# The second expert stage of a two-layer transformer kernel: float32 weights unsplit, two 64-column groups, 18 landing buffers

## The chip, the core and the metric

The kernel runs on one core of one Trainium2 chip. The metric is the device time of one execution in microseconds (us); lower is better. The core has a matrix engine (TensorE, PE in the profile, its weight loads as PEld), a vector engine (DVE), a scalar engine (ACT), GpSimd (POOL) and a queue engine (SP) that issues most DMAs. All of them run at once and wait for each other by semaphores.

## The reference

Two blocks run one after the other. The first has two layers (`DEPTH = 2`), each a mixer and then a mixture of 16 experts in which every expert picks its own tokens. In the second layer only the 512 latent tokens go through the experts, so each of the 16 experts takes 64 tokens of width 1024:

```python
def expert_choice_ffn(h, w_router, w_g, w_u, w_d):
    B, n, D = h.shape
    cap = CAPACITY_FACTOR * n // N_EXPERTS          # 2 * 512 / 16 = 64
    ...
    gate, idx = lax.top_k(aff, cap)
    xs = h[bi, idx]
    a = jnp.einsum('becd,edf->becf', xs, w_g)       # 1024 x 1024 weights per expert
    u = jnp.einsum('becd,edf->becf', xs, w_u)
    y = jnp.einsum('becf,efd->becd', jax.nn.silu(a) * u, w_d)
    return jnp.zeros_like(h).at[bi, idx].add(y * gate[..., None].astype(y.dtype))
```

Three weight matrices per expert make 48 matrices of 4 MB, 201.3 MB in float32, which are each read once.

## The kernel before

`experts(l, ...)` (L1080) is the expert stage of both layers. In layer 1 (the second) it works thus. The mixer before it has written the normed tokens to DRAM as `h2d` (`ffn_input`, L926: transposes `hpt` L992, ACT copies L998, POOL adds L999, four stores L1000), and `top_k` has made the `route` table on DVE. Then, for each expert:

- `gather` (L1128): an indirect DMA on POOL fetches 128 rows of `h2d` into `xs`. 64 of them are the expert's own tokens, the other 64 rows of the array are not used in this layer.
- `turned` (L1114): 8 PE transposes of 128x128 into PSUM, then an ACT copy to the high part and a DVE subtraction to the low part (both float32r, a rounded 32-bit format that PE multiplies in one pass).
- `product` (L1097): a 1024x1024 matrix comes in four loads of 1 MB (`eraw`, L1102, issued on SP, two rows of 4 KB per partition, 8 buffers in pool `er`). Each load is split by ACT (`eh`, L1105) and DVE (`el`, L1106), and then

```python
                    for i in range(2):
                        k = c * 2 + i
                        for f in range(2):
                            fs = slice(f * 512, f * 512 + 512)
                            self.mm3(ps[:, fs], xh[:, k, :], xl[:, k, :], h[:, i, fs], lo[:, i, fs], k == 0, k == 7)
```

  where `mm3` (L80 to L84) is three matmuls: high by high, high by low, low by high. That is 48 matmuls of 128x512 for each matrix. A load's buffer is free again when DVE has made `el`.
- The order of the products is up(e), gate(e+1), down(e), up(e+1). Between them lie SiLU on ACT (L1221), the product with `pup` on DVE (L1233) and another `turned` for the hidden values (`ath`, `atl`).
- `finish` (L1184) scales the output rows on ACT and DVE (`yp..`, L1142, L1143). After every fourth expert a generator `scatter` (L1150) is put in the background: 8 pieces of 128 output columns, each with 4 matmuls against one-hot matrices (L1165) and one DVE update of the residual `xL` (L1167). One piece runs after each step of later products. After the last piece the second block begins with its own weight loads (`raw`, L92) and products (`d`).

The Tile framework allocates buffers and orders each engine's instructions; every engine runs its own list strictly in order. SP's list holds all weight loads one behind the other, so a load that waits for a buffer holds back all that follow.

Of other code the prediction uses only `first_ada` (L462), whose loops issue 64 matmuls in plain float32 at L478, each of 2 stationary columns and 256 moving columns.

Of the kernel before, what the change touches and what calls it, by code (L numbers as in the profile page):

```python
# [9 lines left out]
F32 = mybir.dt.float32  # L10
# [60 lines left out]
class Kernel:  # L71
# [854 lines left out]
    def ffn_input(self, l, lat, T, x, h2d, row0):  # L926


        nc = self.nc
        i = 0 if lat else 1  # L930
        nt = T // 128
        A, B = self.mcol(l, i, 4), self.mcol(l, i, 3)
        u = self.op.tile([128, 8, T], F32, name="u", tag="o")
        w3 = self.tp.tile([128, 3, 8, NE], F32, name="wr", tag="hn", bufs=4)
        wr, wb = w3[:, 0], w3[:, 1:]
        nc.scalar.dma_start(wr, self.A["w_router"][l].rearrange("(k p) e -> p k e", p=128))
        nc.vector.tensor_mul(wb[:, 0], wr, B[:, :, None].to_broadcast([128, 8, NE]))
        nc.vector.tensor_reduce(wb[:, 1, 0], wb[:, 0].rearrange("p k e -> p e k"), axis=AX, op=ALU.add)
        row = [self.tp.tile([128, 512], F32, name="brow", tag="hn", bufs=4) for _ in range(2)]
        for hf in range(2):  # L940
            pb = self.pt.tile([128, 512], F32, name="bps", tag="t")
            for j in range(4):
                dg = self.sp.tile([128, 128], F32, name="diag", tag="diag", bufs=2)
                nc.vector.tensor_scalar(dg, self.ident, B[:, hf * 4 + j:hf * 4 + j + 1], None, ALU.mult)
                nc.tensor.matmul(pb[:, j * 128:j * 128 + 128], self.ones, dg, start=True, stop=True)
            nc.scalar.activation(row[hf], pb, AF.Copy)
        pb = self.pt.tile([128, 512], F32, name="bps", tag="t")
        nc.tensor.matmul(pb[:, :NE], self.ones, wb[:, 1, 0], start=True, stop=True)
        nc.vector.tensor_copy(wb[:, 1, 1], pb[:, :NE])
        acc = self.tp.tile([128, 512], F32, name="acc", tag="oj", bufs=1)[:, :T]  # L950
        lg = self.po.tile([128, 512], F32, name="o", tag="o")[:, :nt * NE].rearrange("p (t e) -> p t e", e=NE)

        def put(j):
            sq = acc if j == 0 else self.tp.tile([128, 512], F32, name="sq", tag="tmp", bufs=5)[:, :T]
            nc.scalar.activation(sq, x[:, j, :], AF.Square)
            if j:
                nc.vector.tensor_add(acc, acc, sq)
            nc.scalar.activation(u[:, j, :], x[:, j, :], AF.Copy, scale=A[:, j:j + 1])
            for t in range(nt):
                nc.tensor.matmul(lg[:, t], u[:, j, t * 128:t * 128 + 128], wr[:, j, :], start=j == 0 and t == 0,  # L960
                                 stop=j == 7 and t == nt - 1, skip_group_check=True)

        def finish():
            if lat:
                ps = self.ps.tile([128, 1024], F32, name="S", tag="S")
            else:
                ps = self.ps.tile([128, 512], F32, name="S", tag="Sc", bufs=2)
            for t in range(nt):
                nc.tensor.matmul(ps[:, t:t + 1], acc[:, t * 128:t * 128 + 128], self.ones[:, 0:1], start=True, stop=True)
            r = self.sp.tile([128, 4], F32, name="nrc", tag="nrc", bufs=2)  # L970
            self.rstd(r[:, :nt], ps[:, :nt], D)
            halves = self.cp.tile([128, nt // 2, 2, NE], F32, name="aff", tag=f"aff{i}")
            aff = halves.rearrange("p t h e -> p (t h) e")
            for t in range(nt):
                nc.vector.scalar_tensor_tensor(halves[:, t % (nt // 2), t // (nt // 2)], lg[:, t], r[:, t:t + 1], wb[:, 1, 1], ALU.mult, ALU.add)
            mx = self.sp.tile([128, 2, nt], F32, name="mx", tag="mx", bufs=1)
            nc.vector.tensor_reduce(mx[:, 0], aff, axis=AX, op=ALU.max)
            nc.vector.tensor_sub(aff, aff, mx[:, 0, :, None].to_broadcast([128, nt, NE]))
            nc.scalar.activation(aff, aff, AF.Exp)
            nc.vector.tensor_reduce(mx[:, 1], aff, axis=AX, op=ALU.add)  # L980
            nc.vector.reciprocal(mx[:, 1], mx[:, 1])
            nc.vector.tensor_mul(aff, aff, mx[:, 1, :, None].to_broadcast([128, nt, NE]))
            self.aff[i] = halves
            if i == 1 or l == 1:
                for _ in self.top_k(lat):
                    pass
            for t in range(nt):
                tok = self.tp.tile([128, 1024], F32, name="tok", tag="big", bufs=2)
                for hf in range(2):
                    ps = self.pt.tile([128, 512], F32, name="hpt", tag="t")  # L990
                    for j in range(4):
                        nc.tensor.transpose(ps[:, j * 128:j * 128 + 128], u[:, hf * 4 + j, t * 128:t * 128 + 128],  # L992
                                            self.ident)
                    o = tok[:, hf * 512:hf * 512 + 512]
                    if i == l == 0:
                        nc.vector.scalar_tensor_tensor(o, ps, r[:, t:t + 1], row[hf], ALU.mult, ALU.add)
                    else:
                        nc.scalar.activation(o, ps, AF.Copy, scale=r[:, t:t + 1])  # L998
                        nc.gpsimd.tensor_add(o, o, row[hf])  # L999
                nc.gpsimd.dma_start(h2d[row0 + t * 128:row0 + t * 128 + 128, :], tok)  # L1000
        return put, finish

# [76 lines left out]

    def experts(self, l, xL, xCd, h2d):  # L1080
        nc, A = self.nc, self.A
        both = l == 0
        with ExitStack() as es:
            P = lambda n, b, **k: self.pool(es, n, b, **k)
            if both:
                rp, wp, xp, yp, kp = P("er", 5), P("ew", 3), P("ex", 2), P("ey", 2), P("ek", 1)
            else:
                rp, yp, kp, wp, xp = P("er", 8, side="right"), P("ey", 2), P("ek", 1), P("ew", 3), P("ex", 2)
            pa, pu, py, pm = (P(n, 1, space=PSUM) for n in ("pa", "pu", "py", "pm"))
            lat, ctx = self.route[0], self.route[1] if both else None  # L1090
            gidx, pidx, cidx = self.slots(lat, ctx)
            iota = kp.tile([128, TL], F32, name="iota")
            nc.scalar.dma_start(iota, A["k_iota"])
            if both:
                xC = kp.tile([128, 8, TC], F32, name="xCe")

            def product(ps, x, W):  # L1097

# [51 lines left out]
            def scatter(parts, T, x, gt2, last):  # L1150
# [24 lines left out]
                if last:  # L1175
                    r = self.r[T] = self.cp.tile([128, 8], F32, name=f"r{T}", tag=f"r{T}")
                    ps = pm.tile([128, 512], F32, name="nps", tag="d", bufs=2)
                    for c in ((0,) if both else (4,)):
                        cs = slice(c, c + min(4, T // 128))
                        self.fold(ps, [acc[:, i * T:i * T + T] for i in range(2)], cs)  # L1180
                        self.rstd(r[:, cs], ps[:, cs], D)
                        yield

            def finish(e, ps):  # L1184
                q = e // 4
                put(f"yp{e // 2 % 2}", e, ps, slice(64 * (e % 2), 64 * (e % 2) + 64), lat, 2)
                if both:
                    r = (2, 0, 3, 1)[e % 4]
                    put("yc", e, ps, slice(32 * r, 32 * r + 32), ctx, 1)
                if e % 4 == 3:  # L1190
                    parts = [(yl.pop((f"yp{i}", 0)), yl.pop((f"yp{i}", 1)),
                              one_hot(TL, pidx[:, 2 * q + i:2 * q + i + 1], "hot")) for i in range(2)]
                    self.background.append(scatter(parts, TL, xL, self.mcol(l, 0, 5), q == 3))
                    if both:
                        part = (yl.pop(("yc", 0)), yl.pop(("yc", 1)), one_hot(TC, cidx[:, q:q + 1], "hotc"))
                        self.background.append(scatter([part], TC, xC, self.mcol(l, 1, 5), q == 3))

            def run(g, n=4):
                for _ in range(n):
# [8 lines left out]
            for e in range(-1, NE):  # L1208
# [12 lines left out]
                    nc.scalar.activation(s, pga, AF.Silu)  # L1221
                if e + 2 < NE:
                    xn = turned(lambda: gather(e + 2), "xt")
                if both and e < 0:
                    self.tc.keep_in_program_order(nc.gpsimd.dma_start(xC, xCd))
                if e >= 0:
                    pdn = py.tile([128, 1024], F32, name="pdn", tag="y")
# [4 lines left out]
                    run(product(pup, x, A["w_e_up"][l, e + 1]))  # L1232
                    nc.vector.tensor_mul(s, s, pup)  # L1233
            self.drain()
            if both:
                nc.gpsimd.dma_start(xCd, xC)


    def pool(self, es, n, b=1, **k):
# [17 lines left out]
    def first_block(self):  # L1257
# [14 lines left out]
        for l in range(2):  # L1272
            first = l == 0
            with ExitStack() as es:
# [77 lines left out]
                if first:  # L1352
                    with ExitStack() as e1:
# [17 lines left out]
                        xC = self.mixer(0, False, [hh, hl], xCd, mCd, gCd, kvc, sink, xcp, h2d, TL)  # L1371
                        self.drain()
                        nc.gpsimd.dma_start(xCd, xC)
            self.experts(l, xL, xCd, h2d)
        return xL


# [536 lines left out]
```

## Time and profile before

| what | us |
|---|---|
| runs of the kernel | 3712.17, 3712.86, 3717.04 (median 3712.86) |
| the profiled execution | 3711.34 |
| its span, first to last instruction | 3709.5 |
| PE busy in the span | 3537.0 (95%) |
| DVE busy | 2676.9 (72%) |
| ACT busy | 2111.5 (57%) |
| weight split of both expert stages, DVE (L1106, 384 times) | 868.3 |
| weight split of both expert stages, ACT (L1105, 384 times) | 730.0 |

The profile page gives busy time by engine, and the span in 40 slices of 92.7 us, in which a digit is the busy share in tenths. Matmuls overlap in PE's pipeline, so the duration of one matmul record is longer than the distance from its start to the next one's; the distance is what a long row of them costs each. The second expert stage lies in slices 24 to 30.

### The profile page before, as it was taken

How to read it: one execution, taken by the hardware profiler on the slowest of the kernel's cores; microseconds unless marked ns; L12 is line 12 of the kernel's file. 1: busy time of each engine (PE TensorE's matmuls, PEld its weight loads, DVE VectorE, ACT ScalarE, POOL GpSimd, SP SyncE). 2: the span in 40 equal slices, each digit the busy share in tenths (PEclk: the TensorE clock that was granted, in tenths of full speed). 3: DMA queues.
4: the chain of work that ended last, by engine and by line, in shares of the span. 5: the costliest groups of instructions: out<-in, count | busy, mean ns of one | idle time of the engine just before them, and what ended most of it. 6: DMA issues, size and time to landing. Idle time of an engine off the chain costs nothing. (4 is left out here: it accounts for less than half of the span.)

```text
span 3709.5 us, 48861 instructions
## 1 busy us (share of the span) xinstructions
PE 3537.0 (95%) x18658; PEld 2911.0 (78%) x18658; DVE 2676.9 (72%) x3677; ACT 2111.5 (57%) x2750; POOL 292.6 (8%) x329
## 2 busy tenths in 40 slices
PE   8999999998899999899999979999999999989998
PEld 5787777998688888687877768888888887768887
DVE  4786775786799999778767659999995555854444
ACT  4555554565677777556645437777775455733233
POOL 2101100010100000130111020000001000010000
PEclk9999999999899999999999989999999999999999
DMA  6333346567899899623244649999982432234332
GB/s 213 118 97 114 113 130 212 163 192 254 323 363 345 338 371 325 224 88 97 94 130 130 205 180 373 352 374 355 351 303 90 135 86 94 89 122 136 92 96 80
DMA packets 394934, 737.17 MB, mean 199 GB/s; under 512 B 25646, under 2 KB 262172, under 8 KB 392908
## 3 DMA queue, kind: packets, MB, share of 16 engines
q1 hardware_dynamic: 380304, 695.15, 54.7%
q0 software_dynamic: 8304, 37.44, 2.6%
q8 instruction: 146, 2.39, 0.3%
q10 hardware_dynamic: 6092, 1.47, 0.2%
q14 instruction: 88, 0.72, 0.1%
HBM read 687.84 MB, written 46.14 MB: 198 GB/s over the span
## 5 line engine op out<-in xcount | busy, mean ns | idle before, releaser
L1106 DVE TENSOR_TENSOR el<-eraw,eh 128x2048 fp32r<-128x2048 f32 x384 | 868.3, 2288 | 76.5 <-ACT eh L1105 74.6
L1105 ACT ACTIVATE eh<-eraw 128x2048 fp32r<-128x2048 f32 x384 | 730.0, 1918 | 220.9 <-PE pup L84 89.3
L96 DVE TENSOR_TENSOR wl<-raw,wh 128x1024 fp32r<-128x1024 f32 (+2 forms) x423 | 506.2, 1200 | 365.6 <-ACT wh L95 362.1
L95 ACT ACTIVATE wh<-raw 128x1024 fp32r<-128x1024 f32 (+2 forms) x423 | 436.6, 1035 | 483.4 <-PE d L83 305.1
L82 PE MATMUL d<-hh,wh 128*128 128x512 f32 (+1 forms) x1304 | 486.7, 374 | 4.9 <-ACT hh L301 4.3
L83 PE MATMUL d<-hl,wh 128*128 128x512 f32 (+1 forms) x1304 | 486.0, 373 | 0.5 <-DVE hl L302 0.5
L84 PE MATMUL d<-hh,wl 128*128 128x512 f32 (+1 forms) x1304 | 485.6, 373 | 0.4 <-DVE wl L96 0.4
L82 PEld LDWEIGHTS d<-hh,wh 128*128 128x128 f32 x1304 | 246.5, 189 | 45.7 <-ACT hh L301 5.1
L84 PEld LDWEIGHTS d<-hh,wl 128*128 128x128 f32 x1304 | 246.4, 189 | 41.1 <-DVE wl L96 2.3
L83 PEld LDWEIGHTS d<-hl,wh 128*128 128x128 f32 x1304 | 246.4, 189 | 39.9 <-DVE hl L302 2.7
L632 ACT ACTIVATE prob<-S,st 128x768 f32<-128x768 f32 (+3 forms) x176 | 134.6, 765 | 142.7 <-DVE st L630 67.1
L83 PE MATMUL pup<-el,xth 128*128 128x512 f32 x512 | 201.4, 393 | 4.2 <-DVE el L1106 4.1
L82 PE MATMUL pga<-eh,xth 128*128 128x512 f32 x512 | 203.8, 398 | 0.0
L83 PE MATMUL pga<-el,xth 128*128 128x512 f32 x512 | 203.2, 397 | 0.5
L82 PE MATMUL pdn<-eh,ath 128*128 128x512 f32 x512 | 202.0, 395 | 0.0
L84 PE MATMUL pga<-eh,xtl 128*128 128x512 f32 x512 | 201.0, 393 | 0.0
L84 PE MATMUL pdn<-eh,atl 128*128 128x512 f32 x512 | 200.0, 391 | 1.0 <-DVE atl L1125 1.0
L83 PE MATMUL pdn<-el,ath 128*128 128x512 f32 x512 | 200.3, 391 | 0.0
L82 PE MATMUL pup<-eh,xth 128*128 128x512 f32 x512 | 199.7, 390 | 0.0
L84 PE MATMUL pup<-eh,xtl 128*128 128x512 f32 x512 | 199.4, 390 | 0.0
L84 PE MATMUL d<-wh,hl 128*128 128x256 f32 (+1 forms) x528 | 160.2, 304 | 3.8 <-DVE hl L302 3.8
L82 PE MATMUL d<-wh,hh 128*128 128x256 f32 (+1 forms) x528 | 160.6, 305 | 0.3 <-DVE xn L1167 0.2
(515 smaller groups left out, 7742.9 us busy)
## 6 DMA issues: line engine op xcount, KB each, us to landing
eraw<-in_w_e_gate SPq DMA_DIRECT2D x128, 1024.0 KB
eraw<-in_w_e_up SPq DMA_DIRECT2D x128, 1024.0 KB
eraw<-in_w_e_down SPq DMA_DIRECT2D x128, 1024.0 KB
raw<-in_w_in SPq DMA_DIRECT2D x170, 512.0 KB
raw<-in_w_ada SPq DMA_DIRECT2D x80, 512.0 KB
raw<-in_w_ff SPq DMA_DIRECT2D x64, 512.0 KB
raw<-in_w_out SPq DMA_DIRECT2D x32, 512.0 KB
raw<-in_w_branch SPq DMA_DIRECT2D x48, 256.0 KB
```

What stands on the lines that cost most here:

```text
L82: mm(ps, wh, xh, start=first, stop=False, skip_group_check=skip)
L83: mm(ps, wh, xl, start=False, stop=False, skip_group_check=skip)
L84: mm(ps, wl, xh, start=False, stop=last, skip_group_check=skip)
L95: for ins in (nc.scalar.activation(h[:, :n], raw[:, :n], AF.Copy), nc.vector.tensor_sub(l[:, :n], raw[:, :n], h[:, :n])):
L96: nc.vector.tensor_sub(l[:, :n], raw[:, :n], h[:, :n])):
L632: nc.scalar.activation(p, S[:, s0:s1], AF.Exp, bias=nm, accum_out=ls)
L1105: nc.scalar.activation(h, raw, AF.Copy)
L1106: nc.vector.tensor_sub(lo, raw, h)
```

## The change

The expert stage of layer 1 gets a function of its own, `last_experts` (L1234 of the changed kernel). Layer 0 keeps `experts`, whose conditions on the layer fall away.

- Weights are no longer split. `product` (L1252) multiplies the float32 tile as it landed. The 64 tokens of the expert are the stationary operand. The output is one PSUM bank of 128x512: the first 512 output columns in partitions 0 to 63, the other 512 in partitions 64 to 127. The two matmuls of a k (L1263) so use the two halves of the array's columns.
- Landing buffers: 18 (8 in one pool, 10 in another) instead of 8. A partition receives two neighbouring rows of the matrix, 8 KB in one piece; to match, `ffn_input` (L1001 to L1004) permutes the columns in `h2d`, and SiLU and the product with `pup` permute theirs. A buffer is free when PE has read it.
- `pair` (L1267) gathers and turns the tokens of two experts at once, one ACT copy in place of the split; `turned` (L1281) does 4 transposes, not 8.
- `finish` (L1315) puts the high part of the scaled output in one half of the partitions and the low part in the other, so that `scatter` (L1289) needs one matmul per piece; it runs per expert, in two steps of four pieces.

```diff
-                    else:
+                    elif l == 0:
                         nc.scalar.activation(o, ps, AF.Copy, scale=r[:, t:t + 1])
                         nc.gpsimd.tensor_add(o, o, row[hf])
+                    else:
+                        ov = o.rearrange("t (c i p) -> t c i p", c=2, i=2)
+                        pv, rv = (a.rearrange("t (c p i) -> t c i p", c=2, i=2) for a in (ps, row[hf]))
+                        nc.scalar.activation(ov, pv, AF.Copy, scale=r[:, t:t + 1])
+                        nc.gpsimd.tensor_add(ov, ov, rv)
...
+    def last_experts(self, l, xL, h2d):
...
+            raws = [(P("era", 8, side="right"), 8), (P("erb", 10, side="right"), 10)]
+            raws = itertools.cycle([p for p, n in raws for _ in range(n)])
...
+            def product(ps, x, W):
+                for c in range(4):
+                    raw = next(raws).tile([128, 2, 1024], F32, name="eraw")
+                    nc.sync.dma_start(raw, W[c * 256:c * 256 + 256, :].rearrange("(p i) f -> p i f", i=2))
+                    for i in range(2):
+                        k = c * 2 + i
+                        for j in range(2):
+                            nc.tensor.matmul(ps[halves[j], :], x(k), raw[:, i, j * 512:j * 512 + 512], start=k == 0,
+                                             stop=k == 7, skip_group_check=True)
+                    yield
...
+            def scatter(ys, hot, gt2, last):
...
+                for f0 in (0, 4):
+                    pts = [pm.tile([128, 512], F32, name="scp", tag="d", bufs=5) for _ in range(4)]
+                    for m in range(4):
+                        nc.tensor.matmul(pts[m], ys[f0 // 4][:, m * 128:m * 128 + 128], hot, start=True, stop=True)
+                    for m in range(4):
+                        f = f0 + m
+                        nc.vector.scalar_tensor_tensor(xL[:, f, :], pts[m], gt2[:, f:f + 1], xL[:, f, :], ALU.mult, ALU.add)
...
+            def finish(e, ps):
+                ys = []
+                for j, m in enumerate(halves):
+                    y = yp.tile([128, 512], F32R, name="y", tag=f"y{j}")
+                    gt = lat[m, 1, e:e + 1]
+                    nc.scalar.activation(y[m], ps[m], AF.Copy, scale=gt)
+                    nc.vector.scalar_tensor_tensor(y[halves[1 - j]], ps[m], gt, y[m].bitcast(F32), ALU.mult, ALU.subtract)
...
+                self.background.append(scatter(ys, hot, self.mcol(l, 0, 5), e == NE - 1))
...
-            self.experts(l, xL, xCd, h2d)
+            if first:
+                self.experts(l, xL, xCd, h2d)
+            else:
+                self.last_experts(l, xL, h2d)
```

What this does to the lists of the engines. PE, in the middle of the stage, before (`pga` is the accumulator of gate, `ept` the transposed hidden values):

```order
L82 MATMUL pga<-eh,xth 128x512
L83 MATMUL pga<-el,xth 128x512
L84 MATMUL pga<-eh,xtl 128x512
L1122 MATMUL ept<-ident,sa 128x128 x2
L82 MATMUL pga<-eh,xth 128x512
```

and one whole expert of the changed kernel (`apt` is the transposed hidden values, `pga`, `pdn`, `pup` are gate of the next expert, down of this one and up of the next, `scp` the scatter):

```order
L1284 MATMUL apt<-ident,s 128x128 x4
L1263 MATMUL pga<-eraw,xt 64x512 x16
L1263 MATMUL pdn<-eraw,at 64x512 x16
L1263 MATMUL pup<-eraw,xt 64x512 x4
L1296 MATMUL scp<-hot,y 128x512 x6
L1263 MATMUL pup<-eraw,xt 64x512 x4
L1296 MATMUL scp<-hot,y 128x512 x2
L1263 MATMUL pup<-eraw,xt 64x512 x8
```

A matrix is 16 matmuls in place of 48, the transposes stand in front of the gate product in place of inside it, and 8 scatter matmuls stand in every expert.

DVE, the same part, before (`el` is the low part of a weight load):

```order
L1106 TENSOR_TENSOR el<-eraw,eh 128x2048 x4
L1143 SCALAR_TENSOR_TENSOR yp1l<-pdn,route_20640,yp1h 64x1024
L1106 TENSOR_TENSOR el<-eraw,eh 128x2048 x3
L1233 TENSOR_TENSOR sa<-sa,pup 128x1024
L1106 TENSOR_TENSOR el<-eraw,eh 128x2048 x2
L1125 TENSOR_TENSOR atl<-ept,ath 128x512
```

and after, one whole expert:

```order
L1360 TENSOR_TENSOR s<-s,pup 128x512
L1322 SCALAR_TENSOR_TENSOR y<-pdn,route_20640,y 64x512 x2
L1299 SCALAR_TENSOR_TENSOR xn<-scp,mod_73,xn 128x512 x8
L1325 TENSOR_SCALAR hot<-iota,route_20640 128x512
L1360 TENSOR_TENSOR s<-s,pup 128x512
```

The split has gone, and 8 residual updates (`xn`) stand in each expert, where there were 8 for four experts.

SP at the end of the stage, before:

```order
L1102 DMA eraw<-in_w_e_up 128x2x1024 x4
L1102 DMA eraw<-in_w_e_down 128x2x1024 x4
L92 DMA raw<-in_w_in 128x3x128 x6
L1699 DMA x2d<-xn 128x4096
L92 DMA raw<-in_w_in 128x3x128 x18
```

and after:

```order
L1259 DMA eraw<-in_w_e_up 128x2048 x4
L1259 DMA eraw<-in_w_e_down 128x2048 x4
L92 DMA raw<-in_w_in 128x3x128 x8
L1827 DMA x2d<-xn 128x4096
L92 DMA raw<-in_w_in 128x3x128 x16
```

The order of the loads is the same; the second block's first loads (`raw`) still stand behind the last expert's.

## Rows read from the trace of the kernel before

**Rows 1.** The page: the span, and GB/s moved in its 40 slices.

```profile
span 3709.5 us, 48861 instructions
...
GB/s 213 118 97 114 113 130 212 163 192 254 323 363 345 338 371 325 224 88 97 94 130 130 205 180 373 352 374 355 351 303 90 135 86 94 89 122 136 92 96 80
```

**Rows 2.** Busy time by stretch: us, engines busy (instructions), granted PE clock, DMA share, GB/s.

```profile
2189.00:2216.00 27.00, 9.43 (x35) 7.64 (x36) 16.34 (x42) 9.89 (x8) 10.18 (x8) 0.57 0.56 201
2216.00:2772.00 556.00, 555.77 (x2563) 459.72 (x2562) 508.72 (x306) 413.12 (x278) 19.27 (x13) 1.00 0.95 356
2600.00:2650.00 50.00, 50.00 (x234) 41.16 (x232) 45.54 (x28) 38.76 (x28) 4.65 (x2) 1.00 1.00 381
```

**Rows 3.** PE in order of time, steady part: start us, us, line, operation.

```profile
2694.68 0.39 PE L82 MATMUL pup<-eh,xth 128*128 128x512 f32 x1
...
2705.56 0.39 PE L82 MATMUL pga<-eh,xth 128*128 128x512 f32 x1
...
2711.01 1.03 PE L1122 MATMUL ept<-ident,sa 128*128 128x128 f32 x8
```

**Rows 4.** Groups by line and shape, 2150 to 2860 us: count, busy us, mean ns, idle before.

```profile
L1106 DVE TENSOR_TENSOR el<-eraw,eh 128x2048 fp32r<-128x2048 f32 x192 | 434.7, 2289 | 43.4 <-ACT eh L1105 42.2
L1105 ACT ACTIVATE eh<-eraw 128x2048 fp32r<-128x2048 f32 x192 | 364.8, 1918 | 115.4 <-PE pup L84 50.3 <-PE pga L84 31.8 <-PE pdn L84 27.6
L1167 DVE SCALAR_TENSOR_TENSOR xn<-scp,mod,xn 128x512 f32<-128x512 f32 x28 | 20.1, 746 | 1.8 <-PE scp L1165 1.7
L1143 DVE SCALAR_TENSOR_TENSOR yp0l<-pdn,route,yp0h 64x1024 fp32r<-64x1024 f32 x8 | 10.2, 1280 | 0.1
L1142 ACT ACTIVATE yp1h<-pdn,route 64x1024 fp32r<-64x1024 f32 x8 | 8.9, 1114 | 11.1 <-PE pdn L84 11.1
L999 POOL TENSOR_TENSOR tok<-tok,brow 128x512 f32<-128x512 f32 x8 | 10.0, 1271 | 0.9 <-ACT tok L998 0.8
```

**Rows 5.** Waits of SP, 2060 to 2860 us: total us, times, longest.

```profile
SPq L1102 <- DVE el L1106: 506.7, 180, 41.0
```

**Rows 6.** PE, SP, POOL and DVE around the stage's start, in order of time.

```profile
2201.08 17.42 SPq L1102 DMA_DIRECT2D eraw<-in_w_e_gate  x4
...
2186.94 1.24 PE L992 MATMUL hpt<-ident,u 128*128 128x128 f32 x8 [2.35 <-ACT tok L998]
...
2193.30 0.56 POOL L1000 DMA_DIRECT2D h2d<-tok  x1 [0.30 <-POOL tok L999]
2198.81 3.16 POOL L1130 DMA_INDIRECT xs<-h2d,gidx  x1 [4.94 <-DVE gidx L1077]
...
2207.63 1.94 PE L1122 MATMUL ept<-ident,xs 128*128 128x128 f32 x8 [11.10 <-DMA xs<-h2d,gidx]
2209.40 0.79 PE L82 MATMUL pga<-eh,xth 128*128 128x512 f32 x1
2209.99 0.63 PE L83 MATMUL pga<-el,xth 128*128 128x512 f32 x1
2210.42 0.63 PE L84 MATMUL pga<-eh,xtl 128*128 128x512 f32 x1
```

**Rows 7.** PE around the stage's end, in order of time.

```profile
2775.92 1.09 PE L1122 MATMUL ept<-ident,sa 128*128 128x128 f32 x8 [1.31 <-DVE sa L1233]
...
2789.06 0.39 PE L84 MATMUL pdn<-eh,atl 128*128 128x512 f32 x1
...
2797.12 0.38 PE L82 MATMUL d<-wh,hh 128*128 128x384 f32 x1
```

**Rows 8.** Plain float32 matmuls of L478: all records, then a run of them in time.

```profile
L478 PE MATMUL d<-wada,cs x128: 377/379/631, 17.2 to 60.3; 128*2 128x256 f32 x128
...
53.32 4.48 PE L478 MATMUL d<-wada,cs 128*2 128x256 f32 x20
```

**Rows 9.** Busy time by stretch, start of the span (columns as in rows 2).

```profile
53.30:57.80 4.50, 4.50 (x22) 1.69 (x22) 0.95 (x1) 1.43 (x2) 0.00 (x0) 1.00 0.31 98
...
10.00:30.00 20.00, 15.56 (x69) 7.70 (x68) 6.62 (x19) 6.99 (x14) 4.45 (x8) 0.86 1.00 351
```

More of the change, by code (lines that the diff above doesn't have):

```diff
@@ L1081, in experts @@
         nc, A = self.nc, self.A
-        both = l == 0
         with ExitStack() as es:
             P = lambda n, b, **k: self.pool(es, n, b, **k)
[L1085 to L1088, printed above, removed]
+            rp, wp, xp, yp, kp = P("er", 5), P("ew", 3), P("ex", 2), P("ey", 2), P("ek", 1)
             pa, pu, py, pm = (P(n, 1, space=PSUM) for n in ("pa", "pu", "py", "pm"))
-            lat, ctx = self.route[0], self.route[1] if both else None
+            lat, ctx = self.route[0], self.route[1]
             gidx, pidx, cidx = self.slots(lat, ctx)
@@ L1093, in experts @@
             nc.scalar.dma_start(iota, A["k_iota"])
-            if both:
-                xC = kp.tile([128, 8, TC], F32, name="xCe")
+            xC = kp.tile([128, 8, TC], F32, name="xCe")
             def product(ps, x, W):
@@ L1177, in scatter @@
                     ps = pm.tile([128, 512], F32, name="nps", tag="d", bufs=2)
[L1178 to L1182, printed above, removed]
+                    cs = slice(0, T // 128)
+                    self.fold(ps, [acc[:, i * T:i * T + T] for i in range(2)], cs)
+                    self.rstd(r[:, cs], ps[:, cs], D)
+                    yield
             def finish(e, ps):
@@ L1186, in finish @@
                 put(f"yp{e // 2 % 2}", e, ps, slice(64 * (e % 2), 64 * (e % 2) + 64), lat, 2)
-                if both:
-                    r = (2, 0, 3, 1)[e % 4]
-                    put("yc", e, ps, slice(32 * r, 32 * r + 32), ctx, 1)
+                r = (2, 0, 3, 1)[e % 4]
+                put("yc", e, ps, slice(32 * r, 32 * r + 32), ctx, 1)
                 if e % 4 == 3:
@@ L1193, in finish @@
                     self.background.append(scatter(parts, TL, xL, self.mcol(l, 0, 5), q == 3))
-                    if both:
-                        part = (yl.pop(("yc", 0)), yl.pop(("yc", 1)), one_hot(TC, cidx[:, q:q + 1], "hotc"))
-                        self.background.append(scatter([part], TC, xC, self.mcol(l, 1, 5), q == 3))
+                    part = (yl.pop(("yc", 0)), yl.pop(("yc", 1)), one_hot(TC, cidx[:, q:q + 1], "hotc"))
+                    self.background.append(scatter([part], TC, xC, self.mcol(l, 1, 5), q == 3))
             def run(g, n=4):
@@ L1223, in experts @@
                     xn = turned(lambda: gather(e + 2), "xt")
-                if both and e < 0:
+                if e < 0:
                     self.tc.keep_in_program_order(nc.gpsimd.dma_start(xC, xCd))
```

87 lines of the change are left out of this document (85 added, 2 removed).

## The prediction

> **What bounds the kernel now.** I read the page first, for the place: the second expert stage is the stretch of 350 to 374 GB/s in slices 24 to 30 of 40 [rows 1], so about 2216 to 2790 us of the span. Then I read that stretch by engine [rows 2]. Between 2216 and 2772 us PE is busy for 555.8 of 556 us, with the granted clock at 1.00 (the 2.4 GHz level), while DVE has 508.7 and ACT 413.1. PE is therefore the bound of this stage. But the last two columns say that the next bound is near: the DMA engines are 0.95 busy at 356 GB/s, and in an undisturbed piece 1.00 busy at 381 GB/s. Where does PE's time go? In order of time [rows 3] the 48 matmuls of an up product start at 2694.68 and the next product starts at 2705.56: 10.88 us per matrix, 0.227 us per matmul. Eight transposes take 1.03 us. Per expert that is 3 x 10.88 + 2 x 1.03 + 8 scatter matmuls x 0.227 = 36.5 us, and 16 experts give 584 us; the trace has the stage's first product at 2209.4 [rows 6] and the last matmul of its last product at 2789.1 [rows 7], 579.7 us, so the account closes to 1%. SP, which issues the loads, waits 506.7 us for DVE's split to free one of the 8 buffers [rows 5]: the loads are held back by the consumer, not the other way round.
>
> **What the change removes.** 192 splits on DVE at 2.289 us and on ACT at 1.918 us, 434.7 and 364.8 us [rows 4]. Neither engine is the bound, so this gives nothing by itself; it unties the buffers from DVE.
>
> **PE's new work.** A matrix is now 16 plain float32 matmuls of 512 moving columns. The trace has such matmuls with 256 columns: the loop of L478 issues 64, and the trace has 128 records [rows 8], so each is two passes. Twenty records in a row take 4.48 us, the last of them 0.38, so (4.48 - 0.38) / 19 = 0.216 us from start to start, at clock 1.00 although only 2 stationary columns are in use [rows 9]. With 512 columns a record is 0.431 us, a matmul two of them, and a matrix 32 x 0.431 = 13.8 us if nothing overlaps. That is more than the 10.88 us of now. The change lives on the two column groups working at the same time: 6.9 us if they overlap fully. PE issues in order, first both passes of group 0, then both of group 1; the second pass of one group can still run beside the first pass of the other, so full overlap is possible in this order. No row here shows two groups side by side, so the ends are 6.9 and 13.8 us. I take 6.9: the two matmuls share no column, no output partition and no weights, and a pass that reads one float32 column per two clock cycles (0.216 us for 256 columns) leaves room for a second at the rate at which the split matmuls read (0.227 us for 512). The Trainium skill, in "TensorE: Matmul & The Clock Gate", Part 3, says that matmuls in different column groups run concurrently and gives 2.38 times for three groups; no row of before shows it. By that efficiency two groups would give 1.59 times, 8.7 us a matrix and 31.8 us an expert where full overlap gives 26.4 below, both under the loads' time, so the end would be the same.
>
> The rest of PE's time per expert: 8 transposes 1.03 us [rows 3], 8 scatter matmuls 1.8 us, a wait of 1.31 us for DVE's product at the transposes, as the last expert has today [rows 7] and as now every expert has, since the transposes stand in front of the next product; and two scatter matmuls beyond the free PSUM banks wait for residual updates of 0.746 us [rows 4], at most 1.5 us. Sum 5.7 us, and 3 x 6.9 + 5.7 = 26.4 us per expert against 36.2 now.
>
> **The loads become the bound.** An expert brings 12.58 MB of weights and 0.26 MB of gathered tokens (one gather for two experts). At the 381 GB/s of rows 2 that is 33.7 us, more than 26.4. Rows of 8 KB in place of 4 KB should raise the rate a little: an engine needs 4096 / (381 / 16) = 172 ns for 4 KB now; a stretch with mostly 1 KB rows moved 351 GB/s at share 1.00 [rows 9], so at least 47 ns for 1 KB; the line through both gives 339 ns for 8 KB, 387 GB/s. I take 385; the ends are 375 (356 / 0.95 [rows 2], no gain from longer rows) and 398 (if the small rows cost more than that stretch shows).
>
> **When the stream starts.** Eight loads are prefetched during the mixer in both kernels. Today the ninth waits for the first split, until 2201.1 [rows 6]. Now two more go when the mixer's last weights are used, and eight more after the last `hpt` transpose, which ends at 2188.2. These eight need 22 us at 385 GB/s, until 2210; then all 18 buffers are full and the stream waits for PE's first step. The path to it is unchanged: route, gather at 2198.8, transposes at 2207.6, first product at 2209.4 [rows 6]. I add 3 us for a gather that now shares the engines with loads, and 3.4 us for the first buffer: four pairs of records at 0.86 us, twice 0.431, because the first matmuls today start 0.43 us apart instead of 0.227 (2209.99 to 2210.42; that is the 1.2 GHz level, and the granted clock from 2189 to 2216 is 0.57 [rows 2]). So from 2216 the stream runs without a pause, since PE is faster and 18 buffers cover its waits of a few us. The strided copies in `ffn_input` are bounded by nothing (POOL's last store is issued at 2193.3, 4.5 us before the gather's indices are there) and by a doubling of 8 POOL adds of 1.27 us [rows 4], 10 us, of which some 8 would delay the gather; I take nothing, by the slack.
>
> **The end.** Left at 2216 are 174 loads (182.5 MB) and 7 gathers (3.7 MB), 186.1 MB, at 385 GB/s 483 us: the last byte lands at 2699. PE then needs the last buffer's work, four pairs of records or 1.7 us, and some delay: last product at 2701.5 instead of 2789.1, **88 us sooner**. From there to the second block's first matmul it is 8 us now [rows 7]. After the change: two half-width ACT copies and DVE subtractions (1.11 / 2 and 1.28 / 2 us [rows 4], 1.2 for the first pair), then 8 residual updates of 0.746 us, 7.2 to 8 us. I take no difference. The second block's loads still stand behind the last weights on SP and land within 2 us of them, while the scatter covers them; if they came later, `d` would be late by as much.
>
> The profiled execution took 3711.3 us (span 3709.5), 1.5 below the median of 3712.9. 3711.3 - 88 = 3623.3, on the median's scale **3625 us**. Rates of 375 and 398 GB/s move the end by +13 and -16 us, a late gather by +8: 3608 to 3650 for this case.
>
> **Rivals.**
> 1. *The column groups do not overlap, or hardly.* For it: no row shows an overlap, and each float32 matmul's two passes stay in one group. Against it: the two have no array column in common. Price: 3 x 13.8 + 5.7 = 47.1 us per expert, 753 us from 2212, end at 2965: 176 us later, about **3889 us**. It decides where a matrix takes more than ((2789 - 2212) / 16 - 5.7) / 3 = 10.1 us, that is below an overlap of 1.36 times; DVE and ACT would be idle and PE full. Chance 0.14.
> 2. *Partial overlap*, 1.36 to 1.5 times (10.1 to 9.2 us): PE stays the bound, the gain is 0 to 45 us, **3665 to 3713 us**. Chance 0.08.
> 3. *PE's clock falls.* With the loads as bound PE pauses at each buffer (1.7 us work in 2.7), and in 2189 to 2216, where PE was busy for 9.4 of 27 us, the clock was 0.57 [rows 2]. Throughout at 1.2 GHz the price is that of the first rival, 3889 us. Against it: at half the clock PE would have no pauses, and full PE has had 1.00. Chance 0.03.
> 4. *The loads are slower than now* because HBM and not the engines limits them: at the 356 GB/s that the stage has on average [rows 2], 186.1 MB take 523 us, end 40 us later, **3665 us**. Against it: 381 GB/s over 50 us. The Trainium skill, in "DMA: Bandwidth & Descriptors", Specifications, has a limit of about 358 GB/s from HBM per core; by it the time would be the same 3665, but the trace's 381 is above that limit already. Chance 0.03.
>
> **How the numbers follow.** The forecast, loads as bound with an overlap of over 1.5 times, has 0.72. The range from 3600 to 3700 holds nearly all of it, the slow loads and the larger half of partial overlap, and leaves out rivals 1 and 3. Changes under 0.2% (7 us) can't be told from none by these measurements. Faster: 0.72 + 0.03 + 0.08 less 0.01 that falls within 0.2%, 0.82; same 0.02, with a little of rival 1 at its edge; slower 0.16.
>
> **What would show it.** Right: from 2220 to about 2695 us a DMA share of 1.00 at 380 to 390 GB/s; the two matmuls of a k overlapping, the eight records of a buffer in about 1.7 us; PE's idle time ended by the loads `eraw`; SP waiting for free lanes, hardly for PE; the clock at 1.00; last `pdn` near 2701 and the same 8 us after it. Wrong: records of L1263 that start 0.43 us apart, one at a time (rival 1), PE without idle time and SP waiting for PE (rivals 1 to 3), a clock near 0.5, or a share of 1.00 at 360 GB/s.

## The result, and the profile after

The changed kernel takes **3588.5 us** (median of 4 runs, 3584.5 to 3590.0) against 3714.2 (4 runs, 3712.2 to 3717.0) for the kernel before on the same chip: ratio 0.9662, 95% interval 0.9649 to 0.9675. It is faster by about 126 us. 3625 was predicted, 88 us faster, in a range from 3600 to 3700: the sign came out and the bound moved as said, but the rate of the loads was mis-sized, and the time lies below the range.

The page of the changed kernel, its span and the GB/s of 40 equal slices, against [rows 1]:

```profile
span 3588.1 us, 46458 instructions
...
GB/s 217 118 100 93 137 121 223 145 167 250 281 364 336 371 333 337 359 106 94 100 108 122 124 246 272 419 419 419 420 345 104 119 93 99 76 125 138 95 95 79
```

The stage is now a flat 419 to 420 GB/s. The same in stretches, against [rows 2] (us; busy us and instructions of PE, PE's weight loads, DVE, ACT and POOL; granted PE clock; DMA share; GB/s):

```profile
2189.00:2216.00 27.00, 3.02 (x12) 2.35 (x12) 10.70 (x46) 2.26 (x4) 8.74 (x9) 0.50 0.92 367
2200.00:2250.00 50.00, 33.45 (x150) 12.41 (x152) 2.14 (x8) 5.33 (x8) 3.87 (x4) 0.78 0.96 391
2216.00:2661.00 445.00, 401.63 (x1748) 134.16 (x1748) 119.08 (x180) 49.02 (x78) 5.62 (x6) 0.99 1.01 416
2400.00:2500.00 100.00, 84.51 (x364) 26.48 (x362) 23.82 (x36) 9.40 (x15) 0.94 (x1) 1.00 1.01 420
2600.00:2650.00 50.00, 42.08 (x180) 12.41 (x176) 8.62 (x13) 3.75 (x6) 0.00 (x0) 1.00 1.01 419
```

PE has fallen from 1.00 busy to 0.84 in the steady part, DVE from 0.91 to 0.27 (119 of 445 us), and the DMA share stands at 1.01 there. The clock is 0.50 at the start and 1.00 in the steady part. Who waits has turned round as well. The waits of SP between 2060 and 2720 us (who is waited for: total us, times, longest us), against [rows 5]:

```profile
SPq L1259 <- DMA eraw<-in_w_e_down: 112.2, 52, 3.0
SPq L1259 <- DMA eraw<-in_w_e_gate: 109.8, 52, 3.1
SPq L1259 <- DMA eraw<-in_w_e_up: 104.2, 49, 3.2
...
SPq L1259 <- PE pga L1263: 29.1, 12, 16.8
```

SP waits 326 us for earlier loads to land and some 50 us for PE; before it waited 507 us for DVE. PE in order of time, at the stage's start, in its steady part and at its end (start us, us, operation, count, idle time before and its releaser):

```profile
2216.55 1.97 PE L1277 MATMUL ept<-ident,xs 128*128 128x128 f32 x8 [17.52 <-DMA xs<-h2d,gpair]
2218.45 9.01 PE L1263 MATMUL pga<-eraw,xt 128*64 128x512 f32 x32
2227.29 7.03 PE L1263 MATMUL pup<-eraw,xt 128*64 128x512 f32 x32
...
2643.09 1.94 PE L1263 MATMUL pdn<-eraw,at 128*64 128x512 f32 x8 [0.45 <-DMA eraw<-in_w_e_down]
2645.61 1.94 PE L1263 MATMUL pdn<-eraw,at 128*64 128x512 f32 x8 [0.58 <-DMA eraw<-in_w_e_down]
2648.20 1.94 PE L1263 MATMUL pdn<-eraw,at 128*64 128x512 f32 x8 [0.65 <-DMA eraw<-in_w_e_down]
...
2661.45 0.66 PE L1284 MATMUL apt<-ident,s 128*128 128x128 f32 x4 [0.79 <-DVE s L1360]
2662.86 7.29 PE L1263 MATMUL pdn<-eraw,at 128*64 128x512 f32 x32 [0.75 <-ACT at L1286]
2672.20 1.49 PE L1296 MATMUL scp<-hot,y 128*128 128x512 f32 x4 [2.05 <-DVE y L1322]
2674.07 2.80 PE L1296 MATMUL scp<-hot,y 128*128 128x512 f32 x4 [0.38 <-DVE y L1322]
2678.78 0.69 PE L82 MATMUL d<-wh,hh 128*128 128x384 f32 x1 [1.91 <-ACT hh L301]
```

The 32 records of a matrix take 7.03 us, and in the steady part a buffer's eight records take 1.94 us and start 2.5 us apart, each time after a short wait for its load. The last product ends at 2662.86 + 7.29 = 2670.2, where before it ended at 2789.5 [rows 7]: 119 us sooner. The second block's first `d` is 118.3 us sooner (2797.12 to 2678.78) and the span 121.4 us shorter. So the gain lies in this stage, and the question is why it is 119 us there and not 88. (The 121 us of the span and the 126 of the medians agree: the profiled run of before lies 2.8 us below its median, that of the changed kernel 1.4 above. What takes the last 3 us behind `d` was not looked into.)

### The profile page after: what moved, and what is told of

Same layout as the page of the kernel before. It is cut to its first block, busy times and chain, and to the rows that moved or that the text cites. A ratio compares the mean times of both kernels' runs of the same rounds, so it can differ in the third digit from the quotient of the medians.

```text
span 3588.1 us, 46458 instructions
## 1 busy us (share of the span) xinstructions
PE 3367.5 (94%) x17753; PEld 2571.7 (72%) x17762; DVE 2268.6 (63%) x3542; ACT 1732.4 (48%) x2542; POOL 273.2 (8%) x321
## 5 line engine op out<-in xcount | busy, mean ns | idle before, releaser
L1106 DVE TENSOR_TENSOR el<-eraw,eh 128x2048 fp32r<-128x2048 f32 x192 | 433.7, 2286 | 33.8 <-ACT eh L1105 33.2
L1105 ACT ACTIVATE eh<-eraw 128x2048 fp32r<-128x2048 f32 x192 | 365.3, 1918 | 106.2 <-PE pup L84 39.1
L83 PE MATMUL d<-wl,hh 128*128 128x256 f32 (+1 forms) x528 | 159.8, 303 | 0.3 <-DVE wl L96 0.3
L628 DVE TENSOR_REDUCE st<-S 128x1 f32<-128x768 f32 (+3 forms) x176 | 137.1, 782 | 22.9 <-PE S L693 20.6
L648 ACT ACTIVATE pth<-ppt 128x512 fp32r<-128x512 f32 x184 | 106.0, 595 | 75.3 <-PE ppt L645 71.5
L649 DVE TENSOR_TENSOR ptl<-ppt,pth 128x512 fp32r<-128x512 f32 x184 | 122.5, 684 | 27.3 <-ACT pth L648 26.3
L1263 PE MATMUL pdn<-eraw,at 128*64 128x512 f32 x512 | 119.0, 599 | 21.2 <-DMA eraw<-in_w_e_down 16.5
L645 PE MATMUL ppt<-ident,prob 128*128 128x128 f32 x736 | 121.7, 277 | 6.8 <-DVE prob L637 6.3
L1263 PE MATMUL pup<-eraw,xt 128*64 128x512 f32 x512 | 119.9, 600 | 6.2 <-DMA eraw<-in_w_e_up 6.2
L1263 PE MATMUL pga<-eraw,xt 128*64 128x512 f32 x512 | 119.2, 607 | 2.9 <-DMA eraw<-in_w_e_gate 2.8
```

The source lines that it names most:

```text
L83: mm(ps, wh, xl, start=False, stop=False, skip_group_check=skip)
L628: nc.vector.tensor_reduce(nm, S[:, s0:s1], axis=AX, op=ALU.max, negate=True)
L645: nc.tensor.transpose(pt[:, h * 128:h * 128 + 128], probs[h], self.ident)
L649: nc.vector.tensor_sub(pl, pt, ph)
L1105: nc.scalar.activation(h, raw, AF.Copy)
L1106: nc.vector.tensor_sub(lo, raw, h)
```

## The experiments

The gap is one term: the loads ran at 419 GB/s, not 385. At first three readings stood beside each other: (A) the pieces of 8 KB are worth far more than the line through two rows of before said; (B) 18 buffers keep the queue full where 8 did not; (C) ACT's and DVE's splits of every buffer had slowed the transfers into the same memory. After the first four runs a fourth was added, (D): the kernel before never showed the limit, since its stream was held back by its consumer and the share of 1.00 there was no measure of what the engines could move. Besides, PE's 7.0 us per matrix was to be shown as an overlap of two column groups. All windows below have the columns of the stretches above, and the brackets behind a ratio are its 95% interval against the kernel before on the same chip.

### Rows of 4 KB again

```diff
-raw, W[c * 256:c * 256 + 256, :].rearrange("(p i) f -> p i f", i=2)
+raw, W[c * 256:c * 256 + 256, :].rearrange("(i p) f -> p i f", i=2)
```

with the order of the columns of tokens and `s` put back to match.

> The changed kernel with one thing undone: each partition again receives two rows of 4 KB that lie 128 rows apart, not one piece of 8 KB (the permutations of the columns go with it). Theory A (the loads are faster because the pieces are longer): DMA share 1.00 at 375 to 385 GB/s in the stage instead of 419; 186.1 MB then take 44 us more than at 419, so about 3632 us. Theory B (the deeper buffers keep the queue full) and theory C (DVE and ACT no longer split, so nothing competes for the on-chip memory): 415 to 420 GB/s and 3588 us as the changed kernel.

Measured: 3600.3 us (3595.0 to 3604.0), ratio 0.9688 [0.9672, 0.9704].

```profile
2400.00:2500.00 100.00, 82.12 (x352) 25.54 (x348) 23.82 (x36) 8.76 (x14) 0.94 (x1) 1.00 1.03 409
```

Rows of 4 KB run at 409 GB/s here, where the kernel before had 381 between 2600 and 2650 with the same rows. The length of the pieces is worth 10 GB/s and 12 us; 28 GB/s have another cause. A explains a quarter of the 38 GB/s.

### Eight buffers

```diff
-raws = [(P("era", 8, side="right"), 8), (P("erb", 10, side="right"), 10)]
+raws = [(P("era", 8, side="right"), 8)]
```

> The changed kernel with 8 landing buffers in place of 18. Theory B: the rate in the steady stage falls towards 375 to 385 GB/s, SP waits for PE again, 3630 us or more. Theories A and C: 415 to 420 GB/s in the steady stage; only the ten loads that are fetched ahead before PE's first step are lost, 10.5 MB or 25 us, less the 8 or so in which the queue stood still with all 18 full, so 3605 to 3613 us.

Measured: 3607.2 us (3606.2 to 3611.5), ratio 0.9711 [0.9694, 0.9727].

```profile
2189.00:2216.00 27.00, 11.51 (x41) 6.18 (x41) 12.98 (x54) 3.72 (x6) 12.36 (x13) 0.52 0.47 152
...
2400.00:2500.00 100.00, 85.40 (x374) 27.99 (x372) 28.01 (x43) 10.44 (x17) 1.87 (x2) 1.00 1.01 419
```

With as many buffers as before the steady rate is the same 419 GB/s. B falls for the rate; the ten further buffers are worth 19 us because they take loads ahead of the first product (367 GB/s against 152 in 2189 to 2216; from 2100 to 2250 the changed kernel moves 6.8 MB more, 16 us at 419 GB/s).

This run has a second use. SP waits for PE here in most of the stage, although the stream runs at its full rate (waits of SP from 2060 to 2720 us, then waits of PE for loads from 2300 to 2600 us):

```profile
SPq L1259 <- PE pga L1263: 169.0, 64, 48.7
SPq L1259 <- PE pup L1263: 128.1, 60, 4.1
SPq L1259 <- PE pdn L1263: 117.8, 60, 2.5
...
PE pdn L1263 <- DMA eraw<-in_w_e_down: 20.4, 32, 1.3
PE pup L1263 <- DMA eraw<-in_w_e_up: 6.8, 11, 0.7
PE pga L1263 <- DMA eraw<-in_w_e_gate: 3.3, 6, 0.6
```

SP's 415 us for PE come from having few buffers; PE itself waits for loads, 30.5 us in these 300. So a queue that waits for its consumer doesn't show by itself that the consumer sets the rate. What shows it is that the consumer, in turn, never waits for a load.

### The order of the two column groups

```diff
-for i in range(2):
-    k = c * 2 + i
-    for j in range(2):
+for j in range(2):
+    for i in range(2):
+        k = c * 2 + i
```

> The changed kernel with the two loops over column group and over k exchanged: in each buffer two matmuls of group 0, then two of group 1. If groups overlap only where the list puts them next to each other, the eight passes of a buffer take 7 places of 0.431 us where they take 4 now: 12.1 us a matrix, 41 us an expert, more than the loads need; PE becomes the bound, the stage ends about 204 us later, 3790 us. If PE picks matmuls of the free group out of a longer queue, or if the overlap isn't what makes a matrix 7 us, the time stays at 3588 us.

Measured: 3591.0 us (2 runs), ratio 0.9668 [0.9648, 0.9687]. In order of time:

```profile
2227.94 7.09 PE L1263 MATMUL pup<-eraw,xt 128*64 128x512 f32 x32
```

A matrix takes 7.09 us with four records of one group in a row, 7.03 with two. The prediction's picture, in which the second pass of one group runs beside the first of the other and so on in strict turn, would have lost overlap here; it fell. The overlap is the same in these two orders; how PE brings it about is not shown.

### Rows of 16 KB

Nine buffers of 2 MB, four rows of a matrix in one piece, a matrix in two loads (`i=4`, `c=1`, `run(g, 2)`).

> The changed kernel with 9 loads in flight of 2 MB, four neighbouring rows per partition (16 KB in one piece), same bytes of buffer. Theory A with a fixed cost per piece (172 ns for 4 KB, 313 ns for 8 KB, so 595 ns for 16 KB): 441 GB/s, 22 us less, 3567 us. If the rate of 419 GB/s is a ceiling of another kind: 419 GB/s and 3588 to 3593 us, since the first and the last step wait for twice as many bytes.

Measured: 3588.7 us (3584.0 to 3589.5), ratio 0.9658 [0.9642, 0.9674].

```profile
2200.00:2250.00 50.00, 30.50 (x136) 11.37 (x138) 2.31 (x9) 5.33 (x8) 3.87 (x4) 0.74 0.86 357
...
2400.00:2500.00 100.00, 84.82 (x382) 29.30 (x380) 24.38 (x36) 9.26 (x15) 0.94 (x1) 1.00 1.01 427
```

The rate rises once more, to 427 GB/s, but the coarse steps give it back: the stream pauses at the start (0.86 and 357 GB/s where the changed kernel has 0.96 and 391) until PE has freed a buffer of twice the size. At these rates a piece takes 16 x 4096 / 409 = 160 ns of an engine's time at 4 KB, 313 at 8 KB, 614 at 16 KB: nearly in proportion.

### One column group

```diff
-nc.tensor.matmul(ps[halves[j], :], x(k), ..., start=k == 0, stop=k == 7, skip_group_check=True)
+g = j if k == 0 else 0
+nc.tensor.matmul(ps[halves[g], :], x(k), ..., start=k == 0, stop=k == 7 or g == 1, skip_group_check=True)
```

> The changed kernel with 14 of the 16 matmuls of a matrix sent to the same 64 columns of the array (both matmuls of the first k stay apart; the later ones of the second output half are added into the first half, so the products are other numbers). Theory, the 7.0 us of a matrix come from two groups working side by side: 28 records at 0.43 us one after the other and four side by side, about 13 us a matrix, 3 x 13 + 5.7 = 44.7 us an expert, the stage is bound by PE, 16 x (44.7 - 30.0) = 235 us more, about 3825 us, and the DMA share falls to about 0.70 at 290 GB/s. Rival, a float32 record with 64 columns takes 0.21 us by itself: a matrix stays at 7 us and the time at 3588.

Measured: 3816.5 us (3813.8 to 3819.2), ratio 1.0273 [1.0254, 1.0292], slower than the kernel before. In order of time, and a stretch:

```profile
2339.66 7.08 PE L1264 MATMUL pga<-eraw,xt 128*64 128x512 f32 x16
...
2347.70 12.66 PE L1264 MATMUL pdn<-eraw,at 128*64 128x512 f32 x31
```

```profile
2300.00:2400.00 100.00, 100.00 (x263) 33.66 (x262) 16.06 (x24) 6.79 (x11) 0.94 (x1) 1.00 0.84 305
```

Sixteen records now take 7.08 us where the changed kernel's take half, and a product 12.7 us. The loads and the other engines' work are the same, so the 7.0 us come from two groups side by side, and without them the change would have lost 103 us. The second line already speaks for D: at 305 GB/s the share is 0.84, where bytes in proportion (305 / 419 x 1.01) would give 0.74.

### The splits beside the loads

```diff
+h = wp.tile([128, 2, 1024], F32R, name="eh", tag="eh")
+lo = wp.tile([128, 2, 1024], F32R, name="el", tag="el")
+nc.scalar.activation(h, raw, AF.Copy)
+nc.vector.tensor_sub(lo[:, 0], raw[:, 0], h[:, 0])
```

> The changed kernel with a copy by ACT of every buffer (1.92 us) and a subtraction by DVE over half of it (1.15 us) beside the products, into scratch tiles that nobody reads, and 12 landing buffers in place of 18 to make room. If ACT's and DVE's work on the buffers slows the transfers (what the kernel before had): the rate in the steady part falls from 419 to about 390 GB/s at a share near 1.00, 12.5 MB an expert in 32.3 us in place of 30.0, about 3630 us. If it does not: 419 GB/s, and only the early loads that have no buffer are lost, 3597 to 3608 us.

Measured: 3612.2 us (3610.1 to 3614.4), ratio 0.9721 [0.9706, 0.9736].

```profile
2200.00:2250.00 50.00, 29.26 (x130) 11.45 (x132) 22.76 (x51) 26.34 (x20) 5.73 (x7) 0.72 0.75 290
...
2400.00:2500.00 100.00, 84.81 (x372) 28.58 (x370) 73.37 (x81) 82.39 (x57) 1.87 (x2) 1.00 1.01 419
```

ACT is 0.82 busy and DVE 0.73 with reads of every buffer and writes beside it, and the loads still come at 419 GB/s. C falls, for splits of this amount (the kernel before had DVE at 0.91). The 24 us lie elsewhere: the first line shows 290 GB/s at the start where the changed kernel has 391, 5 MB or 12 us less between 2200 and 2250 (8 MB or 19 us less between 2100 and 2250), since there are six buffers fewer, and a buffer now also waits for ACT and DVE. That was expected to cost 9 to 20 us and cost a little more.

### Six matmuls of a matrix in one group, rows of 4 KB

The 4 KB version, with:

```diff
-nc.tensor.matmul(ps[halves[j], :], x(k), ...)
+g = 0 if 0 < k < 4 else j
+nc.tensor.matmul(ps[halves[g], :], x(k), ...)
```

> The changed kernel with 4 KB rows (as in the run with two 4 KB rows per partition, 3600 us) and six of the 16 matmuls of a matrix, those of k = 1 to 3, all in one column group (they are added into the first output half, so the products are other numbers). If groups work side by side: 6 x 0.86 + 10 x 0.44 = 9.6 us a matrix, 34.4 us an expert, PE bound as in the kernel before, 12.5 MB in 34.4 us are 365 GB/s, about 3665 us. Then the share tells: 0.92 or so (365 / 409 x 1.03) if the engines' busy time goes with the bytes, as in this kernel at its limit; 0.95 to 1.00, as in the kernel before at 356 to 381 GB/s, if a stream that is held back by its consumer shows more busy time per byte than a free one. With the first, the kernel before paid for ACT's and DVE's splits; with the second, its share simply was no measure of what the engines could move.

Measured: 3658.6 us (3656.8 to 3660.4), ratio 0.9848 [0.9830, 0.9866].

```profile
2400.00:2500.00 100.00, 97.63 (x337) 34.49 (x335) 24.09 (x36) 8.87 (x14) 0.94 (x1) 1.00 1.00 386
2500.00:2600.00 100.00, 97.63 (x340) 34.47 (x339) 24.09 (x36) 10.06 (x16) 0.94 (x1) 1.00 0.99 380
```

and SP's waits from 2060 to 2720 us:

```profile
SPq L1259 <- PE pga L1264: 150.9, 60, 14.7
SPq L1259 <- PE pup L1264: 146.2, 58, 4.3
SPq L1259 <- PE pdn L1264: 110.3, 56, 3.3
```

and PE's only wait from 2300 to 2600 us:

```profile
PE apt L1285 <- DVE s L1361: 5.5, 7, 0.8
```

This reproduces the row of 381 GB/s from which the prediction took its rate. The rows of 4 KB and 18 buffers are those of the first experiment, which ran at 409 GB/s; there is no split. Only PE is slower: it waits for no load (in the kernel before it waits for nothing at all in these 300 us), SP waits 407 us for it, and the DMA share is 0.99 to 1.00 at 380 to 386 GB/s, nearly what the kernel before showed (1.00 at 381). So **D holds**: a stream that is held back by its consumer shows a share of about 1.00 below the rate that it reaches when nobody holds it back. PE's time per expert was a little under the expectation (experts started 31.6, 34.3 and 32.5 us apart between 2333.3 and 2431.7, 32.8 on average, instead of 34.4), so the test stands nearer to the limit than meant; the run with one group is the same case further from it.

The records of single pieces in the traces, 2400 to 2500 us, say the same of the kernel before itself. Half of its 4 KB pieces took 159 ns or less, against 164 in the free stream of the first experiment, although DVE was busy 0.91 of the time with splits. Only its mean is longer, 173 ns against 164: 4% of its pieces took over 1.2 times the median (0.1% in the free stream). In the run with six matmuls in one group the median is 160 ns and 3% are that long; with one group it is 309 ns for 8 KB (313 in the changed kernel) and 12%. So the splits did not slow the pieces at large, which was left open for C (whether they added to the long ones, 4% against 3% without splits, is not shown), and the added busy time of a held-back stream sits in a few long pieces.

### Nine and nine buffers

```diff
-raws = [(P("era", 8, side="right"), 8), (P("erb", 10, side="right"), 10)]
+raws = [(P("era", 9, side="right"), 9), (P("erb", 9, side="right"), 9)]
```

> The changed kernel with the 18 buffers cut 9 and 9 in place of 8 and 10, so that nine loads may go during the mixer. If the ninth has room that early: 1 MB at 419 GB/s sooner, 2.5 us, about 3586 us, at the edge of what the runs can tell. If the space comes free only with the others: 3588.

Measured: 3589.3 us (5 runs, 3585.4 to 3591.4), ratio 0.9661 [0.9648, 0.9674]: the same as the changed kernel. Its profile has 381 GB/s between 2189 and 2216 in place of 367, and its last product starts at 2661.95 instead of 2662.86, 0.9 us sooner and not 2.5. No version tried here is measurably faster than the changed kernel.

## Why the prediction was right or wrong

**Right: the bound moves from PE to the loads.** PE was to need 26.4 us per expert. While it works off the full buffers and waits for little, the down products of three experts start 23.9 and 26.5 us apart:

```profile
2242.88 7.09 PE L1263 MATMUL pdn<-eraw,at 128*64 128x512 f32 x32
...
2266.82 7.04 PE L1263 MATMUL pdn<-eraw,at 128*64 128x512 f32 x32
...
2293.30 7.04 PE L1263 MATMUL pdn<-eraw,at 128*64 128x512 f32 x32
```

The loads need 30.0 us (one every 2.5 us, twelve of them), so they are the bound, as said, but by less: 33 us were expected.

**Right: full overlap of the column groups.** 7.03 us per matrix against the 6.9 taken and the 13.8 of the other end; the run with one group gives 7.08 us for half as many records. Rivals 1 and 2 fall by that, although the first was close in its price: 3889 us was worked out, and 3816 is what the run with 28 of 32 records in one group took. The way of overlapping that the prediction gave, the second pass of one group beside the first of the other, is not borne out: the overlap stays when that order is changed (7.09 us). The estimate of 1.59 times, from three groups in the Trainium skill ("TensorE: Matmul & The Clock Gate", Part 3), is not borne out by this trace either: two groups gave 2.0.

**Wrong: the rate, "I take 385; the ends are 375 and 398".** This step failed, both in its value and in its ends. It took "1.00 busy at 381 GB/s" for what the engines can move. That was PE's own pace: a matrix of 4.19 MB in 10.88 us [rows 3] is 385 GB/s, so a stream that feeds this PE moves no more, whatever the engines can do. The change then had to win everything through longer rows, for which a line through a row of other transfers gave a few GB/s (that row's 351 GB/s [rows 9] is a mean too, over slices of 0.5 us from 78 to 551). The runs show 409 GB/s for the same 4 KB rows when PE does not hold them back, and 419 for 8 KB: of the 38 GB/s above 381, 28 were there before and only hidden, and 10 come with the longer rows (6 were worked out for them). 186.1 MB at 385 GB/s are 483 us. In the trace the last load lands at about 2668.1 (issued at 2648.2; a load takes 19.9 us from issue to landing in this part), 452 us after 2216 or 412 GB/s on average: 31 us less. The last product ends 2.1 us after that byte, where 2.5 were predicted. These 31 us are the whole error of the stage.

The trace of before had what was needed. Its stretch from 2400 to 2500 us, as a whole and its GB/s in 40 slices of 2.5 us:

```profile
2400.00:2500.00 100.00, 100.00 (x464) 82.56 (x463) 91.44 (x53) 77.15 (x53) 4.77 (x3) 1.00 0.99 376
```

```profile
GB/s 406 331 324 403 393 280 408 419 377 352 418 411 362 390 372 369 406 403 364 310 375 378 331 364 338 375 415 408 410 410 410 398 408 392 392 285 397 331 326 380
```

and the same stretch of the changed kernel:

```profile
GB/s 421 413 419 419 423 419 429 419 426 419 419 419 419 423 406 419 419 419 419 419 423 419 410 418 428 419 423 419 423 419 413 416 419 419 419 419 423 419 419 423
```

Before, the rate falls and comes back again and again, and for 12 us on end it stands at 408 to 415 (the 27th slice to the 31st). Engines that seem to have no time left at a mean of 376 moved 408 to 415 for part of the same stretch. That spread, with PE busy for 100 of 100 us while SP waited for buffers (506.7 us for DVE in the whole stage [rows 5]), said that the mean at share 1.00 was the consumer's rate. The prediction read the waits in that way for PE's bound and forgot them when it came to the rate.

**The start: later than said, at little cost, and not for the reason given.** The first gather was to lose 3 us to the loads in front of it. The first product starts at 2218.45 instead of 2209.40, 9 us later; PE waits 17.5 us for the gather, where it waited 11.1 before [rows 6]. But the gather itself takes 9.2 us from issue to landing, against 8.7 before. It was issued late, at 2207.28 instead of 2198.81:

```profile
2195.94 0.56 POOL L1005 DMA_DIRECT2D h2d<-tok  x1 [0.30 <-DMA eraw<-in_w_e_gate]
2207.28 1.03 POOL L1270 DMA_INDIRECT xs<-h2d,gpair  x1 [10.78 <-DMA eraw<-in_w_e_down]
```

Its indices were there at 2200.6. It reads `h2d`, and the last store of `h2d`, issued at 2195.94 among the weight loads, took 10.5 us to land, until 2206.4; before it took 3.0 (the DMA page of that one store, changed kernel and before: KB, us from issue to landing):

```profile
h2d<-tok POOLq DMA_DIRECT2D x1, 512.0 KB, 10.5
...
h2d<-tok POOLq DMA_DIRECT2D x1, 512.0 KB, 3.0
```

With eight buffers, where no weight load is issued between 2180 and 2212, that store takes 3.5 us and the gather 4.6. The prediction put nothing for the store. The trace names a load as what POOL waited for; that it was the store is read from the times.

The loads were to fill all buffers and then wait for PE: they do, SP's longest wait for `pga` is 16.8 us. It costs little (376 GB/s from 2216 to 2250, see the range below). The clock at the start was as foreseen: 0.50 in 2189 to 2216, the 1.2 GHz level, and 9.01 us for the first product against 7.03 for the second.

**The end: right within a microsecond.** ACT's copies take 0.68 us and DVE's subtractions 0.75, where 0.56 and 0.64 were taken; from the last product's end to `d` it is 8.6 us, 8 were said. The second block's first weights are issued from 2652.75 on, beside the last expert's loads, and land among them. `d` waits for ACT, which itself waited 1.83 us for one of these weights before; whether that moved `d` was not tried.

**Rivals 3 and 4.** The clock stood at 0.99 from 2216 to 2661 although PE paused at every buffer; rival 3 falls. Rival 4 has no run for it: every version whose loads were the bound ran above 400 GB/s. The limit of about 358 GB/s that the Trainium skill has in "DMA: Bandwidth & Descriptors", Specifications, is not borne out: 419 GB/s over 400 us stand against it.

**The range** reached down to 3600, beyond the 3608 that the fast end of the rate gave. With 419 GB/s in the prediction's own sum, the last byte lands 444 us after 2216 at 2660 and the time is 3586, 2 us below the median that was measured. In the trace that byte lands 8 us later:

```profile
2216.00:2250.00 34.00, 33.45 (x150) 12.41 (x152) 0.69 (x1) 5.33 (x8) 1.87 (x2) 0.91 0.93 376
2250.00:2661.00 411.00, 368.18 (x1600) 121.75 (x1596) 118.39 (x179) 43.69 (x70) 3.75 (x4) 1.00 1.01 419
```

The pause at the start costs (419 - 376) x 34 us = 1.5 MB, 3.5 us. From 2250 to 2661 the rate is 419. The rest is more bytes: by the records of single pieces 17 loads had landed at 2216, where the sum has 18 (1 MB, 2.5 us), and the second block's first weights land among the last loads (an estimate of 2 us, from 0.4 MB of them by then and 367 GB/s in the last 7 us). That the sum with the right rate comes within 2 us all the same is luck: the 3 us won behind `d`, and the 4 us by which the two profiled runs lie off their medians, make up for it.

**What stays open.** Why some pieces of a held-back stream take long was not settled. The runs show only that the stream has more busy time for each byte: a share of 0.84 at 305 GB/s against 0.74 in proportion for 8 KB rows, 1.00 at 386 against 0.97 for 4 KB rows. From issue to landing a load took 7.3 to 8.4 us in the run with six matmuls in one group and 19 to 21 in the free streams with 18 buffers, so fewer loads were in flight; that this is the cause is argued, not shown.

## What to carry to other kernels

Before a forecast moves a stage's bound onto the DMA engines, find out who held the stream. The issuing queue's waits for a consumer are not enough (415 us of them with eight buffers at the full 419 GB/s). If the consumer in turn never waits for a load, as PE before, a share of 1.00 is not the limit, and the rate to use is nearer to the best short slices of that stream (here 408 to 415), or to what its median piece gives (16 x 4096 B in 159 ns are 412 GB/s), than to its mean (381); the same rows ran at 409 when nobody held them. Such a mistake has one sign: a limit taken from a held-back stream is too low, so the range must reach further to the fast side. And a product with 64 columns is worth putting side by side with another one in the other half of the array, even in plain float32: it decided here between 3588 and 3816 us.

## What the runs showed of the hardware beyond that

- Two 64-column groups overlap by a full factor of 2 (7.0 us against 7.08 for half the records), with two or with four records of one group in a row.
- This core's loads from HBM ran at 409, 419 and 427 GB/s with pieces of 4, 8 and 16 KB, for hundreds of us, at a share of 1.01 to 1.03; with ACT at 0.82 and DVE at 0.73 on the same buffers it was still 419.
- A small transfer that is issued among queued loads lands late: the last 0.5 MB store of the tokens took 10.5 us from issue to landing among loads of 1 MB and 14.1 among loads of 2 MB, where it took 3.0 in the kernel before and 3.5 with eight buffers.
- A held-back stream's median piece is as short as a free one's (159 ns against 164 for 4 KB, 309 against 313 for 8 KB); 3 to 12% of its pieces are over 1.2 times as long.
